# Hybrid SSD/attention encoder on one core: a chain's last term moved to another PSUM bank, its steps and the forms of x reordered

## The chip, the cores and the metric

The kernel runs on one core of one Trainium2 chip. The metric is device microseconds of one execution, start to end on that core. The time before is the median of three runs: 1661.33 us (1657.01 to 1661.57).

## The reference

Two layers on x of 256 tokens by 2048 features, each a residual branch after an RMS norm, and a last norm. Layer 1 is a Mamba-2 mixer, layer 2 a forgetting attention with 32 heads of 128:

```python
def forgetting_attention_mixer(h, w_in, b_forget, w_out):
    proj = h @ w_in                      # 2048 -> 4 * 4096 + 32
    q, k, v, z = ...                     # 4096 columns each
    f_logit = proj[..., 4 * E_WIDTH:]
    log_f = jax.nn.log_sigmoid((f_logit + b_forget).astype(jnp.float32))
    cum = jnp.cumsum(log_f, axis=1).transpose(0, 2, 1)
    ...
        logits = jnp.einsum('bqhd,bkhd->bhqk', q[:, q0:q1], k[:, :q1]) * scale
        logits = logits + cum[:, :, q0:q1, None] - cum[:, :, None, :q1]
        p = softmax(causal logits)
        outs.append(jnp.einsum('bhqk,bkhd->bqhd', p, v[:, :q1]))
    o = o * jax.nn.silu(z)
    return o @ w_out

for i in range(DEPTH):
    x = x + mixer[i](rmsnorm(x, norm_w[i]))
return rmsnorm(x, final_norm_w)
```

All inputs and the output are f32.

## The kernel before

**Precision and weights.** A weight matrix comes in pieces of 128 x 1024 (512 KB). A piece is split into a hi part on ScalarE (`act_hi`, L101, tile `wh`) and a lo part on VectorE (`dve_lo`, L107, tile `wl`); activations are split likewise, so a product is three matmuls: hi x hi, hi x lo, lo x hi. Raw pieces live in seven buffers (tag `raw`), hi parts in five, lo parts in four. `run` (L165 and on) works a list of parts: ahead of each part's matmuls it prepares the pieces up to three further ones (`AHEAD`), and behind them come the part's `post` and what `later(n, ...)` has put off by n units. An ordinary part counts one unit (12 matmuls of 512 columns in the attention's blocks), a sum part half a unit. Instructions are then put in order by a scheduler that also gives out buffers, so an engine's final order can differ by some places from the text.

**Blocks of the attention.** For each group `hq` of four heads two blocks are computed, one for q and k, one for v and z (`block_units`, sixteen in all). A block's result is 256 tokens x 1024 columns, in quarters (token half t, left or right 512 columns i). Half of the inner dimension, `KS` = 8 tiles of 128, is done as a 2 x 2 block product with seven multiplications in place of eight (Strassen's idea): seven combinations of x's blocks, made once (`split_form`: `f`, split into `gh`, `gl`; tiles `ghx`, `glx` in the trace), meet seven combinations of the weights. The weights' combinations are built as running sums in SBUF: chain a begins with a plain load (`sum_a`, SP's queue) and is then added to by loads that accumulate (`nc.gpsimd.dma_start(..., accum_op=add)`, L154, POOL's queue) or by VectorE (`sum_a` += `sum_b`, L156); chains b and c likewise. A step of a chain, written here (chain, term), is two sum parts (`p2` = 0, 1) of six matmuls (`mm_sum`, L901), each on one piece. The other half of the inner dimension is done plainly: four L parts for the left columns, four R parts for the right ones (`mm_rest`, L912, 12 matmuls each).

**Banks and reads.** Products gather in five PSUM banks, x, v, y, z and u, from a pool of five. `STEPS` (L870) sets a block's order:

```python
STEPS = (("a", 0, "load", 0, "x"), "L", ("c", 2, "load", 1, "v"), "L",
         ("b", 3, "load", 3, "z"), "L", ("a", 1, "add", 4, "u"), "L", ("a", 3, "b", 5, "x"), "R",
         ("b", 1, "add", 6, "x"), "R", ("a", 2, "add", 2, "x"), "R", "R")
```

Bank x goes on accumulating through (a, 0), (a, 3), (b, 1) and (a, 2), and is read behind each of the four: by ScalarE (`copy`, L889, into tile `qk` or `vz`), VectorE (`add`, L892), ScalarE, VectorE. Matmuls of the next step on x must wait for that read. After the last L part ScalarE copies y and VectorE adds v; after the last R part VectorE adds z and u.

**Between the blocks** the parts of four heads come one unit after another through `later`: transposes of q and k (`pqk`), their split (`qkh`, `qkl`), logits (`psc`), softmax (`dd`, `uu`), transposes of p (`ppt`) and z, values (`po`), close. Heads of a group start nine units apart (six in two groups, two in the last). From group 1 to 5 the output projection of the group before (`out_f`, L287) stands between two groups.

**Entry to the attention.** The last output projection of layer 1 adds into `xs` (L689) in four column parts of two pieces each. One unit after each, `x2_tiles` transposes the new columns (`pxt`, L791) and makes four k tiles of x: hi on ScalarE, lo on VectorE (L109); for the first eight tiles it also makes the form (four subtractions, L230, and the split) at once. Then the forget projection (two parts, L206 and L210, bank `pst`) opens the attention; with it the old pools close, SBUF and PSUM alike, and new ones open.

Of the kernel before, what the change touches and what calls it, by code (L numbers as in the profile page):

```python
# [64 lines left out]
def hybrid_kernel(ctx: ExitStack, tc: tile.TileContext, a):  # L65
# [12 lines left out]
    phase = ExitStack()  # L78
    ctx.enter_context(phase)
    psm = phase.enter_context(tc.tile_pool(name="psm", bufs=4, space=PSUM))  # L80
    psa = phase.enter_context(tc.tile_pool(name="psa", bufs=4, space=PSUM))
# [64 lines left out]
    def prep_sum(u):  # L146
# [3 lines left out]
        if how == "load":  # L150
            u["sums"][name] = wp.tile([P, 1024], F32, tag="raw", name=f"sum_{name}", bufs=RAW)
            nc.sync.dma_start(u["sums"][name], src)
        elif how == "add":
            nc.gpsimd.dma_start(u["sums"][name], src, accum_op=ALU.add)  # L154
        else:
            nc.vector.tensor_tensor(u["sums"][name], u["sums"][name], u["sums"][how], op=ALU.add)  # L156
# [60 lines left out]
    def blocks(f, summed, j):  # L217

        n = 7 if summed else 3
        return f[:, 1:3, :] if j else f[:, 0:n + 1:n, :]  # L220

    def split_form(f, summed, held, g, name):

        n = 4
        if summed:
            n = 7
            a11, a12, a22, n4, s1, s2, s3, a21 = (f[:, m, :] for m in range(8))
            for out, x, y, op in ((s1, a21, a22, ALU.subtract), (s3, a11, a21, ALU.subtract),
                                  (s2, s1, a11, ALU.subtract), (n4, a12, s2, ALU.add)):
                nc.vector.tensor_tensor(out, x, y, op=op)  # L230
        gh = gp.tile([P, 7, P], F32R, tag="gh", name=f"gh{name}")
        gl = gp.tile([P, 7, P], F32R, tag="gl", name=f"gl{name}")
# [260 lines left out]
    def group_units(g):  # L493
# [280 lines left out]
    def to_layer2(n, t):  # L774


        if t == 1:
            if n == 0:
                lay2["x"], lay2["forms"] = xt_split(2), {}
# [3 lines left out]
            if n == 3:  # L783
                later(2, stats2)

    def x2_tiles(k0):
# [7 lines left out]
        if k0 < KS:  # L794
            f = lp.tile([P, 4 * (S + 1)], F32, tag="zs", name="form")
            f = f[:, :8 * P].rearrange("p (m s) -> p m s", m=8)
# [10 lines left out]
        if f is not None:  # L807
            split_form(f, True, lay2["forms"], 0, f"x{k0 // 2}")

    def stats2():  # L810
# [4 lines left out]
        lay2["rst"] = r  # L815
        lay2["rstH"] = rh = cp.tile([P, 2], F32, name="rstH2")
        nc.vector.tensor_scalar(rh, r, 0.5, None, op0=ALU.mult)
        lay2["rstQ"] = rq = cp.tile([P, 2], F32, name="rstQ2")
        nc.vector.tensor_scalar(rq, r, 1.0 / math.sqrt(FD), None, op0=ALU.mult)
# [32 lines left out]

    def enter_attention():
        nonlocal psm, psa
        phase.close()
        psm = phase.enter_context(tc.tile_pool(name="psm2", bufs=5, space=PSUM))
        psa = phase.enter_context(tc.tile_pool(name="psa2", bufs=3, space=PSUM))
# [11 lines left out]
    def block_units(w_s, w_p, out, scale, done):  # L869
# [18 lines left out]
        def copy(name, t, i):  # L888
            nc.scalar.activation(quarter(t, i), ps[name], AF.Copy, scale=scale(i)[:, t:t + 1])  # L889

        def add(name, t, i, op=ALU.add):
            nc.vector.scalar_tensor_tensor(quarter(t, i), ps[name], scale(i)[:, t:t + 1],  # L892
                                           quarter(t, i), op0=ALU.mult, op1=op)
# [11 lines left out]
        def mm_rest(u, n, names):  # L905
            wh, wl = u["w"][n % 2]
            first = [start(name) for name in names]
            for i, w in enumerate((wh, wh, wl)):
                for k2 in range(2):
                    k = KS + 2 * n + k2  # L910
                    for t, name in enumerate(names):
# [3 lines left out]
                                         stop=2 * n + k2 == KT - KS - 1 and i == 2,  # L915
# [18 lines left out]
        for step in STEPS:  # L934
# [333 lines left out]
```

## Time and profile before

| what | value |
|---|---|
| median of three runs | 1661.33 us (1657.01 to 1661.57) |
| the profiled execution | 1663.63 us, its span 1661.8 us |
| granted TensorE clock, mean | 0.990 |
| busy share: PE, VectorE (DVE), ScalarE (ACT), POOL | 97%, 81%, 64%, 10% |
| HBM traffic | 358.60 MB read, 2.20 MB written, 217 GB/s over the span |
| from the first block's (a, 1) to the last block's last R part, by the timeline of PE | 716.8 to 1577.2 us |

Rows of waits read: engine, tile and line that waited, what ended the wait, then us in total, times, the longest. A row of the timeline gives start, duration, engine, line, operation, out<-in, and in brackets the idle time before it with what ended it. A matmul's end is modelled (0.39 us for 512 columns), and the next one starts 0.23 us after it where nothing waits. Time stamps are us from the span's start.

### The profile page before, as it was taken

Reading aid. Unit: us, or ns where it says so; the run is one execution under the profiler, and the core shown is the slowest. Engines: PE = TensorE matmul, PEld = TensorE weight load, DVE = VectorE, ACT = ScalarE, POOL = GpSimd, SP = SyncE. Lnnn points to the kernel's source line nnn. Section 1 sums busy time; section 2 is a strip of 40 time slices with the busy share of each in tenths; the row PEclk is TensorE's granted clock in tenths of the full one; section 3 lists DMA queues with packets and bytes.
Section 4 is the critical chain, followed back from the end, with each engine's and each line's share of the span. In section 5 each row is a group of like instructions: output and inputs, shape, how many; then the busy total and the mean of one; then the engine's idle time right before and its main releaser. Section 6 shows DMA issues by size and latency. Waiting matters only on the chain. (4 is left out here: it accounts for less than half of the span.)

```text
span 1661.8 us, 22688 instructions
## 1 busy us (share of the span) xinstructions
PE 1607.2 (97%) x7862; PEld 1339.0 (81%) x7862; DVE 1341.9 (81%) x2006; ACT 1068.3 (64%) x1610; POOL 164.9 (10%) x214
## 2 busy tenths in 40 slices
PE   8999999999999999899999999999999999999997
PEld 6888888888888888677887788788788788778786
DVE  6898989898988897777877778777777787778786
ACT  7677676767666655745665665665665665666663
POOL 0000201010101010011110110100100101011000
PEclk9999999999999999899999999999999999999999
DMA  9665889688968896478877787786886887789743
GB/s 349 207 205 192 210 253 247 209 221 249 252 198 227 247 235 195 134 202 252 226 196 234 216 233 223 202 241 192 232 229 172 236 239 175 222 239 240 234 158 101
DMA packets 100963, 362.30 MB, mean 218 GB/s; under 512 B 11600, under 2 KB 12240, under 8 KB 100848
## 3 DMA queue, kind: packets, MB, share of 16 engines
q1 hardware_dynamic: 75888, 271.61, 47.2%
q0 software_dynamic: 24960, 89.24, 29.1%
q8 instruction: 62, 1.02, 0.2%
q14 instruction: 53, 0.43, 0.1%
HBM read 358.60 MB, written 2.20 MB: 217 GB/s over the span
## 5 line engine op out<-in xcount | busy, mean ns | idle before, releaser
L101 ACT ACTIVATE wh<-raw 128x1024 fp32r<-128x1024 f32 (+1 forms) x373 | 392.5, 1055 | 201.5 <-PE psa L287 72.2
L107 DVE TENSOR_TENSOR wl<-raw,wh 128x1024 fp32r<-128x1024 f32 (+1 forms) x373 | 452.3, 1218 | 85.7 <-issue 34.0
L101 ACT ACTIVATE wh<-sum_a 128x1024 fp32r<-128x1024 f32 x176 | 186.1, 1058 | 139.6 <-DMA sum_a<-in_wf_s 46.5
L107 DVE TENSOR_TENSOR wl<-sum_a,wh 128x1024 fp32r<-128x1024 f32 x176 | 214.5, 1221 | 47.4 <-PE psy L912 19.7
L206 PE MATMUL pst<-x,wh 128*128 128x512 f32 x736 | 191.4, 400 | 7.6 <-DVE x L109 7.6
L206 PEld LDWEIGHTS pst<-x,wh 128*128 128x128 f32 x736 | 134.8, 190 | 33.8 <-issue 8.4
L101 ACT ACTIVATE wh<-sum_b 128x1024 fp32r<-128x1024 f32 x88 | 93.4, 1061 | 95.7 <-DMA sum_b<-in_wf_s 61.2
L107 DVE TENSOR_TENSOR wl<-sum_b,wh 128x1024 fp32r<-128x1024 f32 x88 | 107.4, 1222 | 51.9 <-ACT wh L101 34.7
L287 PE MATMUL psa<-wh,x 128*128 128x512 f32 x512 | 132.1, 399 | 0.0
L901 PE MATMUL psx<-wh,ghx 128*128 128x512 f32 x256 | 87.1, 422 | 26.2 <-ACT qk L889 13.6
L287 PEld LDWEIGHTS psa<-wh,x 128*128 128x128 f32 x512 | 94.5, 188 | 21.6 <-issue 3.3
L210 PEld LDWEIGHTS pst<-x,wl 128*128 128x128 f32 x736 | 101.1, 191 | 7.4
L210 PE MATMUL pst<-x,wl 128*128 128x256 f32 x736 | 103.4, 283 | 0.0
L912 PE MATMUL psz<-wh,x 128*128 128x512 f32 x256 | 100.0, 391 | 0.0
L912 PE MATMUL psv<-wh,x 128*128 128x512 f32 x256 | 99.8, 390 | 0.0
L912 PE MATMUL psu<-wh,x 128*128 128x512 f32 x256 | 99.7, 389 | 0.0
L912 PE MATMUL psy<-wh,x 128*128 128x512 f32 x256 | 99.6, 389 | 0.0
L154 POOL DMA_DIRECT2D sum_a<-in_wf_s x64 | 56.8, 888 | 287.6 <-DVE wl L107 194.2
L901 PE MATMUL psx<-wl,ghx 128*128 128x512 f32 x256 | 81.7, 401 | 1.3 <-DVE wl L107 1.3
L901 PE MATMUL psx<-wh,glx 128*128 128x512 f32 x256 | 81.8, 401 | 0.0
L101 ACT ACTIVATE wh<-sum_c 128x1024 fp32r<-128x1024 f32 x44 | 46.7, 1061 | 49.4 <-PE psu L912 15.7
L901 PEld LDWEIGHTS psx<-wh,ghx 128*128 128x128 f32 x256 | 43.8, 193 | 40.4 <-ACT qk L889 16.6
(354 smaller groups left out, 3334.9 us busy)
## 6 DMA issues: line engine op xcount, KB each, us to landing
raw<-in_wf_p SPq DMA_DIRECT2D x128, 512.0 KB, 5.0
raw<-in_wm_t SPq DMA_DIRECT2D x90, 512.0 KB, 4.9
raw<-in_wm_z SPq DMA_DIRECT2D x64, 512.0 KB, 5.4
sum_a<-in_wf_s POOLq DMA_DIRECT2D x64, 512.0 KB, 9.2
raw<-in_wf_o SPq DMA_DIRECT2D x64, 512.0 KB, 5.2
sum_a<-in_wm_s POOLq DMA_DIRECT2D x36, 512.0 KB, 6.3
sum_a<-in_wf_s SPq DMA_DIRECT2D x32, 512.0 KB, 6.4
sum_c<-in_wf_s SPq DMA_DIRECT2D x32, 512.0 KB, 4.2
```

Of the source, the lines that this page charges most:

```text
L101: nc.scalar.activation(out, in_, AF.Copy)
L107: nc.vector.tensor_tensor(out, in_, hi.bitcast(F32), op=ALU.subtract)
L154: nc.gpsimd.dma_start(u["sums"][name], src, accum_op=ALU.add)
L206: nc.tensor.matmul(ps, wh[:, k8 * P:k8 * P + P], ktile(v, k).rearrange("p i s -> p (i s)"), start=k == 0, stop=False)
L210: nc.tensor.matmul(ps[:, S:], wl[:, k8 * P:k8 * P + P], ktile(v, k)[:, 0], start=False, stop=k == KT - 1)
L287: nc.tensor.matmul(held[t][:, a:b], act(2 * n + k2, t)[i % 2], w[:, c], start=n == k2 == i == 0, stop=n == n_h - 1 and k2 == 1 and i == 2)
L901: nc.tensor.matmul(ps[name], y[:, form, :], w[:, p * 512:p * 512 + 512], start=first and i == p == 0, stop=p2 == p == 1 and i == 2, skip_g ...
L912: nc.tensor.matmul(ps[name], token(lay2["x"], k, t)[i % 2], w[:, k2 * 512:k2 * 512 + 512], start=first[t] and i == k2 == 0, stop=2 * n + k ...
```

## The change

- A block's steps have a new order, and the fourth step, (a, 2), accumulates on bank y in place of x. Three R parts stand between (a, 3) and (b, 1). ScalarE copies x once after (b, 1), as quarter (1, 0); u is added from that quarter into (1, 1), and y is added last, by VectorE. ScalarE's copy of y is gone, so there are three copies and five adds a block where there were four and five.
- The first block has its own order, `FIRST`: the two forget parts and three L parts come ahead of the sums, and the sums' first three steps go by `p2` first.
- The forms of x are made in `x2_tiles`, but their subtractions and splits come later, one form a unit (`split_form` from `to_layer2`); each form has a tile of its own and seven slots in place of eight.
- PSUM's pools change at the first forget part as before (`enter_banks`); the SBUF pools of layer 1 now close later, ahead of (a, 1) of the first block.
- The first `sum_b` of a block (not of the first block) has a buffer of its own, made room for by `uu` living in `dd` and one `qkh` in place of two.
- Both halves of a block share one scale: q and k 128^-0.25 each, v and z the root of 0.5 each, with tanh's factor changed to fit.

```diff
-    STEPS = (("a", 0, "load", 0, "x"), "L", ("c", 2, "load", 1, "v"), "L",
-             ("b", 3, "load", 3, "z"), "L", ("a", 1, "add", 4, "u"), "L", ("a", 3, "b", 5, "x"), "R",
-             ("b", 1, "add", 6, "x"), "R", ("a", 2, "add", 2, "x"), "R", "R")
+    A0, A1, A3, A2 = (("a", 0, "load", 0, "x"), ("a", 1, "add", 4, "u"), ("a", 3, "b", 5, "x"),
+                      ("a", 2, "add", 2, "y"))
+    B0, B1, C0 = ("b", 3, "load", 3, "z"), ("b", 1, "add", 6, "x"), ("c", 2, "load", 1, "v")
+    STEPS = (A0, C0, "L", B0, "L", "L", A1, "L", A3, "R", "R", "R", B1, A2, "R")
+    FIRST = (0, "L", "L", 1, "L", A0 + (0,), C0 + (0,), B0 + (0,), A0 + (1,), C0 + (1,), B0 + (1,),
+             "L", "enter", A1, A3, "R", "R", "R", B1, A2, "R")
...
                  ("a", 3): lambda: add("x", 0, 1, ALU.subtract),
-                 ("b", 1): lambda: copy("x", 1, 1),
-                 ("a", 2): lambda: add("x", 1, 0)}
+                 ("b", 1): lambda: copy("x", 1, 0)}

         def left():
-            copy("y", 1, 0)
             add("v", 0, 0)

         def right():
             add("z", 0, 1, ALU.subtract)
-            add("u", 1, 1, ALU.subtract)
+            add("u", 1, 1, ALU.subtract, 0)
+            add("y", 1, 0)
             done(held["out"])
...
         if how == "load":
-            u["sums"][name] = wp.tile([P, 1024], F32, tag="raw", name=f"sum_{name}", bufs=RAW)
+            u["sums"][name] = (
+                fp[0].tile([P, 1024], F32, tag="sum", name=f"sum_{name}") if u.get("apart") else
+                wp.tile([P, 1024], F32, tag="raw", name=f"sum_{name}", bufs=RAW))
...
-            a11, a12, a22, n4, s1, s2, s3, a21 = (f[:, m, :] for m in range(8))
-            for out, x, y, op in ((s1, a21, a22, ALU.subtract), (s3, a11, a21, ALU.subtract),
-                                  (s2, s1, a11, ALU.subtract), (n4, a12, s2, ALU.add)):
+            a11, a12, a22, n4, s1, s2, a21 = (f[:, m] for m in range(7))
+            for out, x, y, op in ((s1, a21, a22, ALU.subtract), (s2, s1, a11, ALU.subtract),
+                                  (n4, a12, s2, ALU.add), (a21, a11, a21, ALU.subtract)):
...
             if n == 3:
                 later(2, stats2)
+                for q in range(KS // 2):
+                    later(2 + q, lambda q=q: split_form(
+                        lay2["f"][q], True, lay2["forms"], 0, f"x{q}"))
...
         if k0 < KS:
-            f = lp.tile([P, 4 * (S + 1)], F32, tag="zs", name="form")
-            f = f[:, :8 * P].rearrange("p (m s) -> p m s", m=8)
+            f = lp.tile([P, 4 * (S + 1)], F32, tag=("xa", "xa", "xd", "zs")[k0 // 2],
+                        name="form", bufs=2 if k0 < 4 else 1)
...
-        if f is not None:
-            split_form(f, True, lay2["forms"], 0, f"x{k0 // 2}")
...
-            st["uu"] = uu = fp[0].tile([P, 384], F32, tag="uu", name="uu")
             ps, dd = st["ps"], st["dd"]
+            st["uu"] = uu = dd
...
-    f[0]["enter"] = enter_attention
-    parts += f
+    f[0]["enter"] = enter_banks
     for g in range(G):
-        for block in four_heads(g):
+        for block in four_heads(g, f):
             parts += block
```

What this does to the engines' order is shown at three places (line numbers after the change are up to 20 higher). First PE at the entry, from the last matmul of layer 1's output projection (`psa`); `pst` is the forget projection, `pxt` the transposes of xs. Before:

```order
L287 MATMUL psa_6752<-wl,ghm_1_6488 128x512
L206 MATMUL pst<-x_0_6572,wh 128x512 x4
L206 MATMUL pst<-x_1_6573,wh 128x512 x4
L210 MATMUL pst<-x_0_6572,wl 128x256 x4
L210 MATMUL pst<-x_1_6573,wl 128x256 x4
L791 MATMUL pxt<-cst,xs 128x128 x8
L206 MATMUL pst<-x_2_6574,wh 128x512 x4
```

After, in the same place:

```order
L288 MATMUL psa_6720<-wl,ghm_1_6488 128x512
L795 MATMUL pxt<-cst,xs 128x128 x2
L209 MATMUL pst<-x_0_6572,wh 128x512 x4
L209 MATMUL pst<-x_1_6573,wh 128x512 x4
L213 MATMUL pst<-x_0_6572,wl 128x256 x4
L213 MATMUL pst<-x_1_6573,wl 128x256 x4
L795 MATMUL pxt<-cst,xs 128x128 x6
L924 MATMUL psv<-wh,x_2_6574 128x512
L924 MATMUL psy<-wh,x_2_6574 128x512
```

Two transposes moved ahead of the first forget part, and an L part (psv, psy) stands where the second forget part stood. Second, VectorE at the same time; `x_0` to `x_3` are the k tiles 0 to 15 in fours, `glx` the lo part of a form, `form` its subtractions, `xs` the residual sum. Before, around the last two sums into xs:

```order
L109 SCALAR_TENSOR_TENSOR x_2_6574<-pxt,vec,x_2_6574 128x256
L689 TENSOR_TENSOR xs<-psa_6751,xs 128x512
L107 TENSOR_TENSOR glx_6698<-form,ghx_6697 128x896
L689 TENSOR_TENSOR xs<-psa_6752,xs 128x512
L230 TENSOR_TENSOR form<-form 128x128
L107 TENSOR_TENSOR wl<-sum_a,wh 128x1024
L109 SCALAR_TENSOR_TENSOR x_1_6573<-pxt,vec,x_1_6573 128x256
L812 TENSOR_REDUCE ssqb<-bsq 128x2
L115 TENSOR_SCALAR rst_6888<-ssqb 128x2
L230 TENSOR_TENSOR form<-form 128x128 x2
L109 SCALAR_TENSOR_TENSOR x_1_6573<-pxt,vec,x_1_6573 128x256
```

After:

```order
L110 SCALAR_TENSOR_TENSOR x_1_6573<-pxt,vec,x_1_6573 128x256 x2
L690 TENSOR_TENSOR xs<-psa_6651,xs 128x512
L690 TENSOR_TENSOR xs<-psa_6652,xs 128x512
L108 TENSOR_TENSOR wl<-raw,wh 128x1024 x2
L110 SCALAR_TENSOR_TENSOR x_2_6574<-pxt,vec,x_2_6574 128x256 x2
L108 TENSOR_TENSOR glx_6897<-form,ghx_6896 128x896
L690 TENSOR_TENSOR xs<-psa_6719,xs 128x512
L110 SCALAR_TENSOR_TENSOR x_2_6574<-pxt,vec,x_2_6574 128x256 x2
L690 TENSOR_TENSOR xs<-psa_6720,xs 128x512
L108 TENSOR_TENSOR wl<-raw,wh 128x1024
```

The last pieces of x_1 moved from behind the last sums into xs to ahead of the pair before them. Third, ScalarE in the first block of group 1, from the first piece of (a, 2); `wh` are weight pieces, `uu` and `dd` the softmax, `ph`, `p` and `qkh` of the heads, `qk<-psx` the copy of bank x behind (b, 1). Before:

```order
L101 ACTIVATE wh<-sum_a 128x1024
L1035 ACTIVATE uu,psum__7890<-uu,mx 128x128
L1035 ACTIVATE uu,psum__7890<-uu,mx 128x256
L101 ACTIVATE wh<-sum_a 128x1024
L1042 ACTIVATE uu<-uu,psum__7890 128x128
L1042 ACTIVATE uu<-uu,psum__7890 128x256
L101 ACTIVATE wh<-raw 128x1024 x2
L889 ACTIVATE qk_7629<-psx,rst_6888 128x512
L101 ACTIVATE wh<-sum_a 128x1024
```

After:

```order
L102 ACTIVATE wh<-sum_a 128x1024
L1062 ACTIVATE dd<-dd,psum__7887 128x128
L1062 ACTIVATE dd<-dd,psum__7887 128x256
L102 ACTIVATE wh<-sum_a 128x1024
L102 ACTIVATE wh<-raw 128x1024
L102 ACTIVATE ph<-ppt 128x256
L102 ACTIVATE wh<-sum_a 128x1024
L1082 COPY p_7947<-ppt 128x128
L102 ACTIVATE qkh_2_7986<-pqk 128x512
L102 ACTIVATE wh<-sum_a 128x1024
L900 ACTIVATE qk_7627<-psx,rstQ_6855 128x512
```

The copy stood behind the two pieces of (a, 2) and two R pieces; it now stands behind the two pieces of (a, 2), one R piece and the first two pieces of the next block's chain a.

More of the change, by code (lines that the diff above doesn't have):

```diff
@@ L217, in blocks @@
     def blocks(f, summed, j):
-        n = 7 if summed else 3
-        return f[:, 1:3, :] if j else f[:, 0:n + 1:n, :]
+        return f[:, 1:3] if j else f[:, 0:7:6] if summed else f[:, 0:4:3]
     def split_form(f, summed, held, g, name):
@@ L944, in block_units @@
                 continue
-            chain, term, how, form, name = step
-            for p2 in range(2):
-                u = {"chain": (chain, w_s[p2, term], how), "sums": sums[p2], "w": [None]}
+            chain, term, how, form, name = step[:5]
+            for p2 in step[5:] or range(2):
+                u = {"chain": (chain, w_s[p2, term], how), "sums": sums[p2], "w": [None],
+                     "apart": chain == "b" and p2 == 0 and order[0] is STEPS}
                 parts.append({"u": u, "h": [0], "long": 1,
@@ L950, in block_units, with four_heads @@
                                   mm_sum(u, form, name, p2)})
-            if (chain, term) in reads:
+            if p2 == 1 and (chain, term) in reads:
                 parts[-1]["post"] = reads[chain, term]
+        if "enter" in order[0]:
+            parts[entering]["enter"] = enter_attention
         return parts
-    def four_heads(hq):
+    def four_heads(hq, first=()):
         st = {}
@@ L1001, in split_qk @@
         def split_qk(i):
[L1002 removed]
+            h = fp[0].tile([P, 512], F32R, tag="qkh", name=f"qkh{hq}_{i}")
             l = fp[0].tile([P, 512], F32R, tag="qkl", name=f"qkl{hq}_{i}")
```

60 lines of the change are left out of this document (35 added, 25 removed).

## Prediction

> **What bounds the kernel now.** I read the page first: engines' shares and the clock.
>
> ```profile
> span 1661.8 us, 22688 instructions
> PE 1607.2 (97%) x7862; PEld 1339.0 (81%) x7862; DVE 1341.9 (81%) x2006; ACT 1068.3 (64%) x1610; POOL 164.9 (10%) x214
> PEclk9999999999999999899999999999999999999999
> ```
>
> TensorE (PE) is busy nearly throughout, and the matmuls are the same before and after. So the change can only win back time in which PE stands still or runs at a lower clock (one slice of the clock row shows 8). The waits of PE tell where that is: first of the stretch with the sixteen attention blocks (716.8 to 1577.2 us), then of everything ahead of it, where the largest is one wait at the entry to attention.
>
> ```profile
> PE psx L901 <- ACT qk L889: 13.6, 8, 2.4
> PE psx L901 <- ACT vz L889: 8.3, 8, 2.1
> PE psx L901 <- DVE vz L892: 2.2, 4, 0.7
> PE psx L901 <- DVE qk L892: 2.1, 4, 0.7
> PE psx L901 <- DVE wl L107: 1.3, 1, 1.3
> ...
> PE pst L206 <- DVE x L109: 7.6, 1, 7.6
> ```
>
> All but 1.3 us of the blocks' 27.5 us are waits of bank x for a read of that same bank: sixteen for ScalarE's copy (L889), one a block, and eight for VectorE's sum (L892). Weights (wl) hold PE once. The timeline of PE at one such place, and then of ACT around it:
>
> ```profile
> 1065.18 0.39 PE L912 MATMUL psz<-wl,x 128*128 128x512 f32 x1
> 1065.41 0.39 PE L912 MATMUL psu<-wl,x 128*128 128x512 f32 x1
> 1067.75 0.95 PE L901 MATMUL psx<-wh,ghx 128*128 128x512 f32 x2 [1.95 <-ACT qk L889]
> ```
>
> ```profile
> 1063.68 1.06 ACT L101 ACTIVATE wh<-sum_a 128x1024 fp32r<-128x1024 f32 x1 [2.25 <-DMA sum_a<-in_wf_s]
> 1064.65 1.04 ACT L101 ACTIVATE wh<-raw 128x1024 fp32r<-128x1024 f32 x1
> 1065.60 0.57 ACT L101 ACTIVATE qkh<-pqk 128x512 fp32r<-128x512 f32 x1
> 1066.07 1.04 ACT L101 ACTIVATE wh<-raw 128x1024 fp32r<-128x1024 f32 x1
> 1067.02 0.68 ACT L889 ACTIVATE qk<-psx,rst 128x512 f32<-128x512 f32 x1
> ```
>
> Matmuls of a dense stretch start 0.23 us apart though each is drawn 0.39 long, so a wait costs PE 0.16 us more than its row says. Here ACT stood 2.25 us for an adding load of sum_a, then made pieces of later steps, and only then the copy that PE waited for: the late sum is felt through the copy queued behind it, not as missing weights. Such waits have a second price, in the clock. In the windows below the columns are PE busy, granted clock, DMA share and GB/s; the first two are the entry, the other five each hold a wait for the copy or the matmuls just behind it.
>
> ```profile
> 684.00:690.00 6.00, 0.00 (x0) 0.65 0.42 76
> 690.00:696.00 6.00, 5.58 (x18) 0.50 0.53 90
> 738.00:744.00 6.00, 4.74 (x14) 0.72 0.50 126
> ...
> 1066.00:1072.00 6.00, 4.25 (x15) 0.72 0.81 230
> 1186.00:1192.00 6.00, 4.93 (x18) 0.72 0.75 242
> 1304.00:1310.00 6.00, 4.21 (x16) 0.75 0.78 244
> 1424.00:1430.00 6.00, 4.96 (x18) 0.72 0.73 221
> ```
>
> **The fourth step to bank y, three R steps ahead of the third.** Before, the third step (b, 1) on x waits for VectorE's read of x one R step earlier, and the fourth (a, 2) for ScalarE's copy of x one R step earlier. After, three R steps lie between the read and the third step: 36 matmuls of 0.23 us, 8.2 us, where one (2.7 us) gave waits of at most 0.7. The fourth step writes to y, whose last matmul is long past and which nothing has read. The copy stands no earlier in ACT's order (behind five weight pieces in the rows above the prediction), but now only the sum of u, after the block's last matmul, needs it. What is taken away:
>
> - waits: 27.5 + 25 x 0.16 = 31.5 us (25 waits);
> - clock: (4 x 0.28 + 0.25) x 6 us = 8.2 us, five windows;
> - together 39.7 us, if nothing takes their place.
>
> The Trainium skill (TensorE: Matmul & The Clock Gate, Part 1) has the clock fall to half only after an idle window of about 3.4 us, and advises against idle gaps over about 3 us. This trace differs: a wait drawn 1.95 us long is followed by a window at 0.72. By the rule the blocks would have nothing to win in the clock, and 31.5 us at most instead of 39.7; I go by the windows.
>
> **What takes their place.** First the sums' loads. Before, this is one block's round: the four adding loads are issued on POOL, and ACT begins the last piece at 1111.86, when its load has landed.
>
> ```profile
> 1094.09 0.87 POOL L154 DMA_DIRECT2D sum_b<-in_wf_s  x1 [17.94 <-DVE sum_a L156]
> 1098.23 0.87 POOL L154 DMA_DIRECT2D sum_b<-in_wf_s  x1 [3.28 <-DVE sum_a L156]
> 1098.83 2.16 POOL L154 DMA_DIRECT2D sum_a<-in_wf_s  x2
> ```
>
> ```profile
> 1111.86 1.06 ACT L101 ACTIVATE wh<-sum_a 128x1024 fp32r<-128x1024 f32 x1 [2.06 <-DMA sum_a<-in_wf_s]
> ```
>
> From the first issue to the last landing: 17.8 us. At 1094.09 PE was just starting the third L step. In the new order there follow that step, a 1, L, a 3, R, R, R, b 1 and half of a 2: 2.7 + 2.75 + 2.7 + 2.75 + 8.2 + 2.75 + 1.4 = 23.2 us to the last piece (a pair of sum steps takes 2.75 us, below). Its lo half is first needed 0.9 us later and takes 1.06 on ACT and 1.22 on VectorE, so the load may land 23.2 + 0.9 - 2.3 = 21.8 us after the first issue: 4.0 us to spare.
>
> ```profile
> 1550.16 2.75 PE psu L901 x12
> ```
>
> ```profile
> 1107.81 0.74 DVE L892 SCALAR_TENSOR_TENSOR vz<-psx,rst,vz 128x512 f32<-128x512 f32 x1
> ...
> 1110.03 1.22 DVE L107 TENSOR_TENSOR wl<-sum_a,wh 128x1024 fp32r<-128x1024 f32 x1
> ```
>
> Second, VectorE. From b 1 to the next block's first L there are now ten pieces in 6 x 2.75 = 16.5 us of PE (b 1, a 2, R, a 0, c, L), and VectorE owes 10 x 1.22 + 3 x 0.74 = 14.4 us for them, with the heads' work on top. At the end z and u are summed ahead of the second piece of c: 2 x 0.74 + 1.22 = 2.7 us of work against the 4.1 us that a 0 and half of c give. Nowhere in the blocks before stand four sum pieces in a row; the price lies between 0 and one such piece, 1.4 us a block. I take 0.5, nearer to nothing, since wl held PE once in all the blocks: 16 x 0.5 = 8 us. Blocks: 39.7 - 8 = 31.7 us.
>
> **The entry.** PE's last matmuls ahead of it and its next; then VectorE's rows in between:
>
> ```profile
> 681.78 1.07 PE L287 MATMUL psa<-wl,ghm 128*128 128x512 f32 x4
> 690.42 0.77 PE L206 MATMUL pst<-x,wh 128*128 128x512 f32 x1 [7.57 <-DVE x L109]
> ```
>
> ```profile
> 684.68 0.68 DVE L689 TENSOR_TENSOR xs<-psa,xs 128x512 f32<-128x512 f32 x1
> 685.28 1.08 DVE L107 TENSOR_TENSOR glx<-form,ghx 128x896 fp32r<-128x896 f32 x1
> 686.28 0.69 DVE L689 TENSOR_TENSOR xs<-psa,xs 128x512 f32<-128x512 f32 x1
> ...
> 689.80 0.48 DVE L109 SCALAR_TENSOR_TENSOR x<-pxt,vec,x 128x256 fp32r<-128x256 f32 x1
> 690.20 0.28 DVE L230 TENSOR_TENSOR form<-form 128x128 f32<-128x128 f32 x1
> ```
>
> PE loses 7.57 + 0.16 = 7.7 us, and then 2.8 more, as the 5.6 us from 690.42 to 696 run at 0.50. VectorE is late there because each tile of x drags its form along (four subtractions of 0.28 and a split of 1.08); x's last piece that PE wants stands at 689.80. After, those pieces of x precede the last two sums into xs, and two L steps stand ahead of the second forget step, so k tiles 12 to 15 get 5.4 us more. Two waits are new. Two transposes now go ahead of the first forget step and wait for the sum into xs: from 0 to the 2.5 us between PE's last matmul (ended at 682.85) and the end of the first sum, 685.36 in the old order; I take 1.5. And the second forget step may wait for tiles 12 to 15, behind a split: 0 to 2, I take 1.5. Entry: 7.7 + 2.8 - 3.0 = 7.5 us.
>
> **At nothing.** One copy a block less: 16 x 0.68 us of ACT, which has 36% idle; it hides behind PE. The same matmuls and as many VectorE operations. The new factors of scale change no instruction. exp's result in place of dd: the next head's dd waits until this head's is transposed, which comes three units later while heads start nine apart; in the last group, two apart, VectorE may stand a step, hidden by the pieces already made, else up to 2.75 us, once or twice. The first block's closer a terms: 0 to 2 us, once. Seven weight buffers now hold three long-lived sums and not four, so one more load can go ahead.
>
> **Sum.** 31.7 + 7.5 = 39.2 us off the profiled execution: 1663.6 - 39.2 = 1624.4. That execution is 2.3 us over the median of the runs, 1661.3; against the median the forecast is 1622. Its own range: with nothing new 1661.3 - 39.7 - 10.5 = 1611; with 1.4 us a block and the entry's gain down to 4.5, 1661.3 - 17.3 - 4.5 = 1639.5.
>
> **Rivals.** *DMA becomes the bound in the blocks.* For it: the second of these windows (last two columns: DMA share and GB/s), from the sums to the fourth step, is full, and closing PE's gaps asks for the same bytes sooner.
>
> ```profile
> 1084.00:1096.00 12.00, 12.00 (x59) 9.99 (x58) 9.06 (x9) 6.75 (x7) 0.87 (x1) 1.00 0.49 153
> 1096.00:1114.00 18.00, 18.00 (x85) 14.84 (x84) 13.24 (x21) 10.88 (x17) 2.63 (x3) 1.00 1.00 256
> ```
>
> Against it: the first window is half empty, and the freed buffer can fill it. If half of the blocks' 39.7 us comes back as waits for weights, 19.8 - 8 + 7.5 = 19.3 us are left: 1642.
>
> *Slower: the last sum lands late.* Four adding loads now feed four sum pieces in a row. If, beside one more load in flight, the 17.8 us of the round grow by 4.0 plus 2.0, PE waits 2.0 us in each block, enough by the windows for a half clock of 0.28 x 6 = 1.7: 16 x 3.7 = 59 us against the 39.7 + 7.5 won, 1673. It decides where the half clock sets in: waits of 1.9 us without it, 16 x 1.9 = 30 us, would be no loss. For it: share 1.00; against it: it needs the round a third longer. The Trainium skill (SBUF — State Buffer, Who interferes with whom) has loads from POOL's queue wait for their descriptors while VectorE, in a two-port mode, holds the port that it shares with POOL; a denser VectorE could then do this. No run here shows it.
>
> *No difference.* The four splits, 4 x (4 x 0.28 + 1.08) = 8.8 us, mostly ahead of the entry before, fall where VectorE is full and eat the entry's 7.5 us; and the blocks' waits move to the next block's first use of banks that z, u and y leave late. Against it: y's bank is wanted 5.5 us after the block's end. About 1660.
>
> **Chances.** Forecast 0.70, DMA 0.18, no difference 0.06, slower 0.06. Less than 0.3% (5 us; the three runs spread over 4.6) can't be told from no change. Faster by more: 0.70 + 0.18 = 0.88; within: 0.06; slower: 0.06. The range takes in the forecast's own from 1610 and the DMA case with 3 us of margin: 1610 to 1645.
>
> **What would show it.** In the new waits of PE the rows of psx for ACT's copy are gone, and psy has none over 0.5; the clock shows no window at 0.72 in the blocks; the entry's wait is under 2 us, with at most a short stretch at 0.50. The DMA case shows as PE waiting for wh or wl at b 1 and a 2 with DMA at 1.00; the slower case as such a wait of 2 us on psy in nearly every block. A wait over 1 us on bank x at b 1 would refute the first step; forms (ghx, glx) holding PE after the entry would refute the price of the splits.

## The result, and the profile after

The changed kernel took 1614.49 us (median of 4 runs, 1612.77 to 1618.07), the kernel before 1660.36 (4 runs, 1657.01 to 1661.57): ratio 0.973, 95% interval 0.9707 to 0.9752, faster by 45.9 us. The forecast was 1622, in a range of 1610 to 1645. The profile of the changed kernel was taken of its slowest execution, 1618.07 us, so its rows lie 3.6 us over the median.

The page of the changed kernel: its span, the engines, the clock row.

```profile
span 1616.3 us, 22668 instructions
PE 1591.6 (98%) x7862; PEld 1333.1 (82%) x7862; DVE 1342.0 (83%) x2006; ACT 1061.6 (66%) x1594; POOL 163.8 (10%) x214
PEclk9999999999999999999999999999999999999999
```

PE executes the same 7862 matmuls, and its busy time is 15.6 us shorter: matmuls at half clock are drawn longer, and there are hardly any left. The span is 45.5 us shorter, so some 30 us are waits. The waits of PE after, from the largest, without those of layer 1:

```profile
PE ppt L1069 <- ACT dd L1062: 2.0, 3, 0.9
PE pxt L795 <- DVE x L110: 1.8, 1, 1.8
...
PE po L1095 <- ACT p L1082: 1.0, 2, 0.8
...
PE psz L924 <- DVE wl L108: 0.3, 1, 0.3
PE psx L913 <- ACT wh L102: 0.2, 1, 0.2
PE psx L913 <- DVE wl L108: 0.2, 1, 0.2
```

The rows of psx for ScalarE's copy and for VectorE's sum are gone, and nothing took their place on y or on the weights: 0.7 us in three waits, all in the first block. The entry, PE's timeline, and then windows of it and of the sixteen blocks from the end of their first loaded sum pieces on (PE busy first; the last three columns are granted clock, DMA share, GB/s):

```profile
684.61 0.41 PE L795 MATMUL pxt<-cst,xs 128*128 128x128 f32 x2 [1.75 <-DVE x L110]
685.11 2.69 PE L209 MATMUL pst<-x,wh 128*128 128x512 f32 x8
```

```profile
683.02:686.43 3.41, 1.73 (x8) 1.30 (x9) 3.41 (x9) 2.19 (x7) 0.00 (x0) 1.00 0.46 177
686.43:689.84 3.41, 3.41 (x15) 3.13 (x14) 2.22 (x13) 1.90 (x2) 0.86 (x1) 0.50 0.46 151
...
710.30:1531.00 820.70, 816.85 (x3858) 678.13 (x3857) 667.68 (x893) 527.21 (x739) 90.74 (x111) 1.00 0.83 231
```

The wait of 7.57 us is 1.75 now, with one window at half clock behind it. VectorE's rows there tell what it is for:

```profile
682.99 0.68 DVE L690 TENSOR_TENSOR xs<-psa,xs 128x512 f32<-128x512 f32 x1
683.60 0.86 DVE L110 SCALAR_TENSOR_TENSOR x<-pxt,vec,x 128x256 fp32r<-128x256 f32 x2
684.38 0.68 DVE L690 TENSOR_TENSOR xs<-psa,xs 128x512 f32<-128x512 f32 x1
```

The first of the two sums into xs ended at 683.67, VectorE's reads of the bank pxt at 684.46, and the transposes start at 684.61: half of the wait is for the sum, the other half for the bank.

In the blocks PE is busy for 816.85 of 820.70 us at full clock. DMA's share there is 0.83 (0.80 in the same stretch before, 716.8 to 1577.2): loads have room left.

The rows of one other engine say where this came from. ScalarE's waits for adding loads between 720 and 1575 us, before, and then after (total, times, longest):

```profile
ACT wh L101 <- DMA sum_b<-in_wf_s: 61.2, 25, 4.9
ACT wh L101 <- DMA sum_a<-in_wf_s: 46.5, 27, 2.8
```

```profile
ACT wh L102 <- DMA sum_a<-in_wf_s: 14.2, 7, 3.3
ACT wh L102 <- DMA sum_b<-in_wf_s: 1.5, 1, 1.5
```

ScalarE stood 107.7 us for late sums before, and 15.7 after. In the kernel before, such a wait lies shortly ahead of every one of PE's sixteen waits for the copy: ScalarE had stood 1.8 to 2.8 us for a load of sum_a, with two more weight pieces and at most two short instructions between that piece and the copy, and in fifteen of the sixteen that was longer than PE then stood. The bank of the fourth step should not change this, since the loads neither read nor write it (the old order on bank y, below, bears that out). So two theories stand against each other. **The bank**, as the prediction argued: PE waits for x to be read, and y needs no reading. **The order**: with the adding loads given more time ScalarE doesn't stand, the copy comes in time, and x would have done as well.

### The profile page after: what moved, and what is told of

The parts are those of the page before. It is cut to its first block, busy times and chain, and to the rows that moved or that the text cites. A ratio compares the mean times of both kernels' runs of the same rounds, so it can differ in the third digit from the quotient of the medians.

```text
span 1616.3 us, 22668 instructions
## 1 busy us (share of the span) xinstructions
PE 1591.6 (98%) x7862; PEld 1333.1 (82%) x7862; DVE 1342.0 (83%) x2006; ACT 1061.6 (66%) x1594; POOL 163.8 (10%) x214
## 3 DMA queue, kind: packets, MB, share of 16 engines
q1 hardware_dynamic: 75888, 271.61, 48.4%
## 5 line engine op out<-in xcount | busy, mean ns | idle before, releaser
L690 DVE TENSOR_TENSOR xs<-psa,xs 128x512 f32<-128x512 f32 (+1 forms) x81 | 51.8, 678 | 26.1 <-PE psa L288 26.1
L288 PE MATMUL psa<-wh,ghf 128*128 128x512 f32 (+1 forms) x260 | 71.3, 394 | 0.0
L288 PE MATMUL psa<-wl,x 128*128 128x512 f32 x256 | 69.4, 391 | 1.2 <-DVE wl L108 1.2
L288 PE MATMUL psa<-wl,ghf 128*128 128x512 f32 (+1 forms) x260 | 69.4, 387 | 0.0
L288 PE MATMUL psa<-wh,glf 128*128 128x512 f32 (+1 forms) x260 | 69.3, 386 | 0.0
```

Of the source, the lines that this page charges most:

```text
L288: nc.tensor.matmul(held[t][:, a:b], act(2 * n + k2, t)[i % 2], w[:, c], start=n == k2 == i == 0, stop=n == n_h - 1 and k2 == 1 and i == 2)
L690: nc.vector.tensor_tensor(c, pss[t][:, a:b], c, op=ALU.add)
```

## The experiments

### Bank and order, one without the other

*The new order, bank x.*

```diff
-                      ("a", 2, "add", 2, "y"))
+                      ("a", 2, "add", 2, "x"))
...
-                 ("b", 1): lambda: copy("x", 1, 0)}
+                 ("b", 1): lambda: copy("x", 1, 1),
+                 ("a", 2): lambda: add("x", 1, 0)}
...
         def left():
+            copy("y", 1, 0)
             add("v", 0, 0)
...
-            add("u", 1, 1, ALU.subtract, 0)
-            add("y", 1, 0)
+            add("u", 1, 1, ALU.subtract)
```

> The changed kernel with its step order, its entry and its splits, but the fourth step (a, 2) on bank x again, right behind the third (b, 1), with the old reads (ScalarE copies x after the third step, VectorE adds x after the fourth, ScalarE copies y after the last L). Theory (the bank is what removes the waits): each block waits again for ScalarE's copy of x, and as no R step lies between now, by the 2.7 us of that step longer than before: 1.4 + 2.7 = about 4.1 us a block, 66 us, and a half-clock window of 1.7 us behind each, 27 us more: 1614 + 66 to 93 = 1680 to 1707 us. Rival (the three R steps ahead of the third do the work, the bank little): within 5 us of the changed kernel's 1614.

Measured: 1619.32 us (0.9761 of before, 0.9736 to 0.9787), only 4.8 us over the changed kernel. The theory of the bank fell. One thing must be read beside it: the scheduler moved half an R step between the third and the fourth, so the copy had 1.4 us and not none. PE's timeline there, and ScalarE's copy:

```profile
868.74 0.61 PE L913 MATMUL psx<-wl,ghx 128*128 128x512 f32 x2
869.20 0.39 PE L924 MATMUL psz<-wh,x 128*128 128x512 f32 x1
...
870.33 0.39 PE L924 MATMUL psu<-wh,x 128*128 128x512 f32 x1
870.68 0.72 PE L913 MATMUL psx<-wh,ghx 128*128 128x512 f32 x2
```

```profile
869.96 0.67 ACT L900 ACTIVATE vz<-psx,rstH 128x512 f32<-128x512 f32 x1
```

The copy starts at 869.96, with no wait of ScalarE for a load in the 10 us ahead of it, and ends at 870.63; PE goes on at 870.68, where matmuls 0.23 us apart would have had it at 870.56, and has lost 0.1 us. So it is in the other blocks, but for one wait of 0.8 us in the second. Before, it lost 1.4 us on average with a whole R step in between.

*Two R steps ahead of the third step and one between it and the fourth, on bank x and on bank y. (In this and the next runs of the order the second half of `FIRST` is changed in the same way, and the runs on bank x have the edits of the reads above.)*

```diff
-STEPS = (A0, C0, "L", B0, "L", "L", A1, "L", A3, "R", "R", "R", B1, A2, "R")
+STEPS = (A0, C0, "L", B0, "L", "L", A1, "L", A3, "R", "R", B1, "R", A2, "R")
```

> As the kernel with bank x only, but with one of the three R steps moved between the third and the fourth step (A3 R R B1 R A2 R), so that the fourth step stands as far behind the copy as before the change. Theory: the sixteen waits for ScalarE's copy return at the old size, 21.9 + 16 x 0.16 = 24.5 us, with 8.2 us of half clock: 1614 + 33 = 1647 us, the eight waits for VectorE stay away (two R steps ahead of the third are enough). Rival (ScalarE is early enough in the new order): 1614 to 1620.

> The same order (A3 R R B1 R A2 R) with the fourth step on bank y: against the changed kernel only one R step moves from ahead of the third step to between third and fourth, and the four sum pieces in a row of the next block become two and two. Theory: no bank is waited for, and VectorE's density costs nothing: 1612 to 1617. Rival (the four pieces in a row cost 0.5 us a block, as the prediction took it): 8 us less, 1606.

Measured: bank x 1617.45 us (0.9752, 0.9724 to 0.9779), bank y 1612.51 (0.9716, 0.9686 to 0.9747). The sixteen waits did not return on x; one of 3.5 us did, in the second block, and it drew a half-clock window. It bears the theory of the order out, for there ScalarE had once more stood for a sum ahead of the copy:

```profile
772.59 1.06 ACT L102 ACTIVATE wh<-sum_a 128x1024 fp32r<-128x1024 f32 x1 [2.76 <-DMA sum_a<-in_wf_s]
...
775.44 0.67 ACT L900 ACTIVATE vz<-psx,rstH 128x512 f32<-128x512 f32 x1
```

```profile
776.16 1.22 PE L913 MATMUL psx<-wh,ghx 128*128 128x512 f32 x2 [3.49 <-ACT vz L900]
```

With a full R step in between, x is worth 4.9 us and not 33. On y, the order with two R steps is as good as the one with three, to the 2 us that these runs can tell, and the 8 us of the rival, four sum pieces in a row, are not there.

*The old order, bank y; and the missing corner, the old order on bank x with the new entry, splits and tiles.*

```diff
-STEPS = (A0, C0, "L", B0, "L", "L", A1, "L", A3, "R", "R", "R", B1, A2, "R")
+STEPS = (A0, "L", C0, "L", B0, "L", A1, "L", A3, "R", B1, "R", A2, "R", "R")
```

> The fourth step on bank y, but the steps of a block in the order of the kernel before (A0 L C0 L B0 L A1 L A3 R B1 R A2 R R); the first block keeps its new start. Theory: of the blocks' 39.7 us the waits for the copy (24.5) and the half clock (8.2) are gone, the eight waits for VectorE and the one for wl, 4.3 + 1.3 + 9 x 0.16 = 7.0 us, stay: 1614 + 7 = 1621. Rival (half clock also follows from the order, or a late sum now holds PE as weights): over 1630. Rival (the order does nothing): 1614.

> The missing corner of the square of bank and order: a block's steps in the order of the kernel before and the fourth step on bank x with the old reads, but the changed kernel's entry, splits and factors. Measured so far: new order with bank y 1614.5, with bank x 1619.3; old order with bank y 1631.3. Theory (bank and order remove the same waits, each most of them, because the copy is late only where ScalarE has stood for a late adding load): the kernel before less its entry, 1661 - 6.5 = 1654, so that the bank is worth 23 us in the old order and 5 in the new. Rival (bank and order add up, and the entry and the splits hold the rest): 1631 + 5 = 1636 us.

Measured: 1631.31 us on y (0.9838, 0.980 to 0.9875) and 1662.85 on x (10 runs, 1656.24 to 1669.89; 1.0007, 0.9985 to 1.003). Both theories missed. On y the time is 10 us over the 1621 that the returning waits for VectorE should give, in the range of the rival in which a late sum holds PE. The longest wait there does come from a late sum, though through VectorE's add and not as a weight: in the second block ScalarE stood for a sum, VectorE for ScalarE's piece and then added x, and PE stood for that add:

```profile
768.75 1.06 ACT L102 ACTIVATE wh<-sum_b 128x1024 fp32r<-128x1024 f32 x1 [4.78 <-DMA sum_b<-in_wf_s]
```

```profile
769.84 1.23 DVE L108 TENSOR_TENSOR wl<-sum_b,wh 128x1024 fp32r<-128x1024 f32 x1 [4.96 <-ACT wh L102]
770.98 0.74 DVE L903 SCALAR_TENSOR_TENSOR vz<-psx,rstH,vz 128x512 f32<-128x512 f32 x1
```

```profile
771.78 0.74 PE L913 MATMUL psx<-wh,ghx 128*128 128x512 f32 x2 [3.82 <-DVE vz L903]
```

On x the time is 8.9 us over the theory's 1654, of which the small edits are a part (the last but one of these runs).

| us, medians | bank x | bank y | the bank |
|---|---|---|---|
| old order | 1662.9 | 1631.3 | -31.6 |
| new order | 1619.3 | 1614.5 | -4.8 |
| the order | -43.6 | -16.8 | |

Bank and order overlap: each alone takes most of the 48.4 us between the corners, and the order alone takes more. The corner of 1662.9 holds up to 7.8 us that small edits cost in the old order, as a later run shows; with 1655.1 in its place the bank is worth 23.8 us there and the order 35.8, if the edits cost nothing in the other corners, which wasn't tried. The finding is the same. The waits for ScalarE's copy in the old order on x, then ScalarE's own waits for the adding loads there, in the old order on y, and in the new order on x:

```profile
PE psx L913 <- ACT qk L900: 13.6, 7, 2.3
PE psx L913 <- ACT vz L900: 6.9, 7, 1.0
```

```profile
ACT wh L102 <- DMA sum_b<-in_wf_s: 53.3, 17, 4.6
ACT wh L102 <- DMA sum_a<-in_wf_s: 44.5, 25, 4.1
```

```profile
ACT wh L102 <- DMA sum_a<-in_wf_s: 53.3, 28, 4.4
ACT wh L102 <- DMA sum_b<-in_wf_s: 44.0, 15, 4.8
```

```profile
ACT wh L102 <- DMA sum_a<-in_wf_s: 12.0, 5, 3.2
ACT wh L102 <- DMA sum_b<-in_wf_s: 2.4, 2, 1.7
```

In the old order ScalarE stands 97.8 us on x and 97.3 on y: the bank leaves the cause alone and takes away the place where PE mostly feels it. In the new order it stands 14.4 us even on x: the cause is gone. The loads have more room: from the issue of a round's first adding load to the first matmul of (a, 2) it is 22.7 us before (median of the blocks, with PE's own wait in it) and 24.8 after. They also land sooner, sum_a's in 7.8 us where it was 9.2 (medians from issue to landing). How much each of the two does was not separated. The timeline of the old order on x shows the link at one place. ScalarE waits for a sum, makes pieces, then the copy; PE waits for that:

```profile
944.20 1.06 ACT L102 ACTIVATE wh<-sum_a 128x1024 fp32r<-128x1024 f32 x1 [2.30 <-DMA sum_a<-in_wf_s]
...
947.54 0.68 ACT L900 ACTIVATE qk<-psx,rstQ 128x512 f32<-128x512 f32 x1
```

```profile
948.27 0.73 PE L913 MATMUL psx<-wh,ghx 128*128 128x512 f32 x2 [2.14 <-ACT qk L900]
```

Without the 2.30 us, and if nothing else had held ScalarE, the copy would have started at about 945.2 and ended before PE got there at 946.

### Which half of the order

> Bank y, the changed kernel's first half of a block (A0 C0 L B0 L L A1 L A3) with the old second half (R B1 R A2 R R). Theory (what counts is the room between step a 3, whose pieces free the sums for the next adding loads, and b 1, which waits for the first of them): as the old order on bank y, 1626 to 1632. Rival (what counts is the first half, the distance from a 0 and b 0 to their next terms): as the changed kernel, 1612 to 1617.

> Bank y, the old first half (A0 L C0 L B0 L A1 L A3) with the new second half as it stood in the run of 1612.5 (R R B1 R A2 R). Theory (the room between a 3 and b 1 counts): 1612 to 1617. Rival (the first half counts): 1626 to 1632.

Measured: new first half with old second half 1619.27 us (0.9749, 0.9725 to 0.9773), old first half with new second half 1613.30 (0.9711, 0.9689 to 0.9732). So the second half, the R steps between a 3 and b 1, does all of it by itself; the first half does most, 12 of the 17 us. The first run met neither of its two ranges. The times between the last matmuls on u of the blocks, from the traces, show where the two differ:

| us | layer 1's last matmul to the first block's end | the other fifteen blocks |
|---|---|---|
| before | 66.5 | 828.1 |
| after | 55.4 | 793.3 |
| old order, bank x | 58.8 | 835.6 |
| old order, bank y | 57.1 | 804.1 |
| old second half, bank y | 58.5 | 790.0 |
| old first half, bank y | 53.2 | 790.2 |
| two R steps, bank y | 54.7 | 789.9 |

In the fifteen blocks either half is enough, to 0.3 us beside the kernel with two R steps (the changed kernel's profile has 3 us of waits for the heads' softmax in them), although ScalarE still stands 63.8 and 64.6 us for sums in them, against 97.3 with both halves old. That such waits cost nothing while they stay under the lead of the pieces is argued from this, not shown. What the old second half loses is in the first block, where a wait of 2.3 us for a piece drew two windows of half clock. The expectation had put everything in the second half, and was half right.

### VectorE's density

```diff
         dve_lo(wl, raw, wh)
+        if u.get("twice"):
+            dve_lo(wl, raw, wh)
...
+                     "twice": (chain, term) in (("b", 1), ("a", 2)),
```

> The changed kernel with VectorE's lo split of the four sum pieces of the third and fourth steps done twice (the second writes the same values again): 4 x 1.22 = 4.9 us more VectorE a block, 78 us in all, where the prediction saw VectorE owe 14.4 us in 16.5 and took 0.5 us a block for it. Theory (pieces are made 3 to 9 us ahead, VectorE makes the time up elsewhere in the block, as it is 81% busy there): up to 5 us more, 1614 to 1620. Rival (VectorE is at its edge there, as the prediction priced it): 14.4 + 4.9 - 16.5 = 2.8 us a block, 45 us, 1659.

Measured: 1612.69 us (0.9709, 0.9683 to 0.9734). The page shows that the work was done:

```profile
PE 1587.4 (99%) x7862; PEld 1331.2 (83%) x7862; DVE 1409.1 (88%) x2070; ACT 1061.9 (66%) x1594; POOL 163.4 (10%) x214
```

64 more instructions and 67 us more of VectorE, and no more time (1.8 us less, within the runs' spread). The eight us that the prediction took for VectorE were not there.

### The entry

*The splits of x's forms early again, all else as in the changed kernel; then the second forget step right behind the first.*

```diff
-                for q in range(KS // 2):
-                    later(2 + q, lambda q=q: split_form(
-                        lay2["f"][q], True, lay2["forms"], 0, f"x{q}"))
...
+        if f is not None:
+            split_form(f, True, lay2["forms"], 0, f"x{k0 // 2}")
```

```diff
-FIRST = (0, "L", "L", 1, "L", A0 + (0,), ...
+FIRST = (0, 1, "L", "L", "L", A0 + (0,), ...
```

> The changed kernel with only the splits of x's forms back where they were (each tile of x drags its four subtractions and its lo split along). Theory (VectorE's splits ahead of x's pieces are what made the entry wait long): the wait at the entry grows from 1.8 toward the 7.6 us of the kernel before, at least to 4, with up to 1.7 us of half clock: 1617 to 1622 us. Rival (the later entry of the attention's buffers and the two L steps ahead of the second forget step won it): within 2 us of 1614.5.

> The changed kernel with the second forget step right behind the first, ahead of the L steps (the scheduler may still move single matmuls). Theory (k tiles 12 to 15 need the time of the two L steps: in the changed kernel the last of them is written at 695.2, 5.1 us after the first forget step's end): a wait of 2 to 5 us and a half-clock window of 1.7, 1616 to 1621 us. Rival (VectorE and the scheduler bring them earlier, so that nothing waits): 1613 to 1615.

Measured: 1619.12 us (0.9766, 0.9748 to 0.9783) and 1616.57 (0.9748, 0.9729 to 0.9767): 4.6 and 2.1 us over the changed kernel. The first interval just touches that of the changed kernel (0.9707 to 0.9752), the second overlaps it. PE's waits with the early splits, and with the forget steps in a row:

```profile
PE pxt L792 <- DVE x L110: 3.7, 1, 3.7
PE pxt L792 <- DVE xs L690: 1.6, 1, 1.6
```

```profile
PE psy L913 <- DVE wl L108: 2.7, 1, 2.7
```

The splits are confirmed: 5.3 us of waits in place of 1.8, and two windows at half clock behind them where there was one. The forget steps are not what the expectation said, though the time fell into its range. PE did not stand at the second forget step, since the scheduler filled it with matmuls of the L steps; the wait came over 40 us later, for a weight piece of the first block's fourth step. VectorE was late with that piece because an instruction of a head stood ahead of it, which waited for a load (cB):

```profile
735.04 0.35 DVE L1040 SCALAR_TENSOR_TENSOR dd<-cB,cum_q,cst 128x128 f32<-128x128 f32 x1 [7.51 <-DMA cB<-cum_d]
735.31 1.22 DVE L108 TENSOR_TENSOR wl<-sum_a,wh 128x1024 fp32r<-128x1024 f32 x1
```

So the range was met by luck, and what k tiles 12 to 15 cost isn't measured.

*The old order on bank x had come out 8.9 us over its expectation. The same with the small edits undone.*

```diff
-"apart": chain == "b" and p2 == 0 and order[0] is STEPS
+"apart": False
...
-st["uu"] = uu = dd
+st["uu"] = uu = fp[0].tile([P, 384], F32, tag="uu", name="uu")
...
-h = fp[0].tile([P, 512], F32R, tag="qkh", ...)
+h = fp[0].tile([P, 512], F32R, tag="qkh", ..., bufs=2)
```

> The kernel with the old order on bank x and the new entry came out at 1662.9 (1656 to 1670), where 1654 was expected: its entry and first block were 7.6 us shorter in the profile, its other fifteen blocks 7.5 us longer. This kernel is the same with the small edits undone too (no extra buffer for sum_b, exp's result in its own tile, two buffers for qkh). Theory (one of these costs in the old order what the entry won): 1654. Rival (they cost nothing, and the longer blocks are waits that move against the clock's windows from run to run): 1656 to 1670 again, with the fifteen blocks at 830 us or more.

Measured: 1655.09 us (12 runs, 1650.3 to 1658.76; 0.9974, 0.9959 to 0.9989). This is the theory's number. In the profiles the fifteen blocks are 5.7 us shorter than in the old order on bank x before (835.6 to 829.9), and the first, with the entry, 3.3. So in the old order the three small edits cost 7.8 us by the medians, 5.5 by the two ratios, whose intervals just touch; about as much as the entry won. Which of the three does it wasn't tried. This kernel differs from the kernel before the change by the entry, the first block's start and the splits alone (and the factors), so its 0.26% (0.11 to 0.41), 4.3 us, are what these are worth by themselves.

*The attention's PSUM pools opened earlier, at the first part of layer 1's last sum into xs, in the order with two R steps.*

```diff
-    f[0]["enter"] = enter_banks
...
+    parts[-2]["enter"] = lambda: enter_banks()
```

> Bank y, two R steps ahead of the third step and one behind it (the run of 1612.5), and the attention's PSUM pools opened one half step's block earlier, ahead of the last sum into xs, so that the entry's transposes and the first forget step find banks that no reader holds. Theory (the 1.9 us left at the entry are a bank's wait, released when VectorE has read pxt): the gap shrinks to about 1.2, the wait for the sum into xs alone, and no half-clock window follows: 0.7 + 1.7 = 2.4 us less, 1610. Rival (the wait is for the sum into xs): 1612 to 1613.

Measured: 1612.84 us (0.9727, 0.9711 to 0.9743), no better than the 1612.51 of the same order without it. At the old place no gap and no half-clock window are left, but the last transposes no longer stand there either, and PE now waits a block of matmuls earlier:

```profile
678.37 0.41 PE L795 MATMUL pxt<-cst,xs 128*128 128x128 f32 x2 [2.00 <-ACT wh L102]
```

The wait moved. The row names a weight piece of ScalarE, which reads no bank, so what PE waits for there is not shown. No kernel of the study is clearly faster than the changed one: the best four lie at 1612.5 to 1613.3, with intervals that overlap its own.

## Why the prediction was right or wrong

- **What bounds the kernel**: right. Only waits of PE and half-clock windows were won; VectorE with 67 us more work changed nothing, and with DMA at 0.83 in the blocks PE waits 0.3 us at most for a weight.
- **What the blocks lose (39.7)**: the size was right. The fifteen blocks after the first are 34.8 us shorter in the profiles (828.1 to 793.3), and the first, with the entry, 11.1.
- **What takes it away**: the step that failed. The prediction said that the copy "stands no earlier in ACT's order" and that bank y takes PE out of its way. It had the rows that showed ScalarE standing for the late sum ahead of the copy, and it worked out that the new order leaves the loads 4.0 us to spare, but did not ask what that does to ScalarE's wait. It removes it: 107.7 us of ScalarE's waits became 15.7, and on bank x, in the new order, the copy is in time but for one wait in each run, of 0.8 and 3.5 us (1619.3 and 1617.5). The bank by itself would have given the forecast's sign too, which is why the time alone could not have told the two apart.
- **VectorE's density (8 us)**: the term that was mis-sized. Measured by doubling the work: nothing. The bound had been taken from the 16.5 us of PE against 14.4 of VectorE in that one stretch; pieces are made ahead (in the first block of the changed kernel the lo pieces of (a, 2) end at 728.1 and 730.8 us and are first used at 733.0 and 734.3), and that this lead carries over the stretch is argued. Without this term the forecast is 1661.3 - 39.7 - 7.5 = 1614.1, against 1614.5 measured; that the two agree so closely is partly luck, as the entry, measured by itself, is worth 4.3 and not 7.5.
- **The entry (7.5)**: near. By itself 4.3 us (0.11% to 0.41%) in the old order; undone in the new one, the splits cost 4.6; the forget step's 2.1 came by another wait. The wait for the two transposes, taken as 1.5 for the sum into xs, is 1.75, half of it for a bank that the prediction did not name, and with a half-clock window behind it, a loss of 1.7 us that was not in the sum. The wait at the second forget step, taken as 1.5, did not come.
- **At nothing**: nearly true in the new order, where three waits for exp's result in dd, 2.0 us together, and two for p, 1.0 (0.5 before), are all that shows; with two R steps there are none of them. In the old order the same edits cost 5.5 to 7.8 us, so their cover there is gone; that it is the new order's room which hides them is argued, not shown.
- **The rivals**: DMA as the bound fell with its share of 0.83 and no wait for a piece above 0.3 us in the blocks; the late last sum fell with ScalarE's 15.7 us of waits for sums. That the splits would eat the entry was refuted; VectorE's room was larger than thought.
- **Its signs**: they came out. No row of psx for the copy is left, none of psy came, and the entry's wait is 1.75 us. They fit the order as well as the bank, so they could not decide between the two.

What stays open: which of the three small edits has a cost in the old order, and why the first half of the order, which leaves a 3 and b 1 as close as before, serves the later blocks as well as the second half does. Nor was it separated how much the loads' room and how much their faster landing does.

## What to carry to other kernels

When PE waits for an engine that works through its instructions in order, as ScalarE does in these timelines, ask what that engine stood for ahead of the instruction that is waited for: here a copy was late because a load was, and either making the load earlier or moving the reader away removes the wait. Two parts of one change that cure the same wait don't add up, so try each alone before giving one the credit. And price an engine's density by what it may lag (the lead of its pieces), not by its busy share in the densest stretch; an extra copy of the suspected work measures it in one run.

## What the runs showed of the hardware

The half-clock windows lie on a fixed grid. The last five of the kernel before start at 740.40, 1068.08, 1187.55, 1307.01 and 1426.48 us by the clock's record in the trace: 96.0 and three times 35.0 steps of 3.413 us apart. What seems to count is how much of one such cell PE stands. Two cells of the kernel before and the ones behind them (PE busy first, clock third from the end):

```profile
1303.60:1307.01 3.41, 1.62 (x7) 1.03 (x7) 3.21 (x4) 3.41 (x5) 0.00 (x0) 1.00 0.79 280
1307.01:1310.42 3.41, 3.41 (x12) 2.94 (x12) 2.22 (x3) 1.45 (x2) 0.00 (x0) 0.50 0.78 210
...
948.62:952.03 3.41, 1.92 (x9) 1.30 (x8) 3.20 (x4) 3.41 (x5) 0.00 (x0) 1.00 0.78 284
952.03:955.44 3.41, 3.41 (x19) 2.88 (x19) 3.05 (x9) 2.06 (x3) 0.66 (x1) 1.00 0.74 219
```

The cell in which PE was drawn busy for 1.62 us is followed by one at half, the cell with 1.92 isn't. There is no sharp limit. Over the fourteen traces, start and end left out, all nineteen cells at full clock in which PE was drawn busy for 1.60 us or less were followed by one at half. Of the nine with 1.62 to 1.78 us four were (in the kernel before, 1.62 us at 1303.60 was and 1.62 us at 781.36 was not), and of those above only three (2.05, 2.10 and 2.29 us). Five windows at half clock stood straight behind another in which PE was drawn busy for 2.6 to 3.4 us; what draws such a second one is not known. So the same wait can be cheap or dear by where it falls: at the entry the changed kernel and the one with the old first half both wait 1.75 us, the first with a half-clock window behind it, as above, the second without one anywhere. The second's wait, and the window behind it:

```profile
683.72 0.41 PE L795 MATMUL pxt<-cst,xs 128*128 128x128 f32 x2 [1.75 <-DVE x L110]
```

```profile
684.40:687.80 3.40, 3.40 (x23) 3.06 (x24) 2.82 (x14) 1.76 (x4) 0.86 (x1) 1.00 0.39 122
```

That is 1.7 us between kernels that do the same there. The Trainium skill (TensorE: Matmul & The Clock Gate, Part 1) says that the clock is judged over a free-running window of 3413 ns; the spacing here agrees. Its advice to avoid idle gaps above about 3 us (same page, Why this matters for your kernels) is too mild for these traces, where 1.8 us of idle drawn within one window was enough every time, and a gap of 2.3 us split over two passed (old order on bank x, ahead of 1304.89 us).
